# Sixteen of the adaLN dot products moved from the projections to the output projection and the down product

## The chip, the cores and the metric

The kernel runs on one core of one Trainium2 chip. The metric is device time in microseconds (us) of one launch. Of TensorE (PE), VectorE (DVE), ScalarE (ACT), GpSimd (POOL) and the queue that SyncE (SP) issues transfers on, each works through its own instruction list in order; a later instruction of a list never passes an earlier one that waits.

## The reference, cut to what matters

The program is one layer: an adaLN-modulated bidirectional mLSTM mixer, then an adaLN-modulated ConvFFN, over 1024 latent tokens of width 1024 with a prefix of 256 context tokens.

```
cx = silu(c)                                     # one row of 1024
sh1, sc1, g1, sh2, sc2, g2 = split(cx @ ada_w + ada_b, 6)     # 6 x 1024 values
hx = rmsnorm(x) * (1 + sc1) + sh1                # needed first of all
yx = mlstm_mixer(hx, hc) @ w_out                 # projections, scan, output projection
x  = x + g1 * rmsnorm(yx)                        # g1 is needed at the end of the output projection
hx = rmsnorm(x) * (1 + sc2) + sh2                # sh2, sc2: before the up product
yx = conv_ffn(hx)                                # up product, gate with convolution, down product
x  = x + g2 * rmsnorm(yx)                        # g2: only at the end of the down product
```

The change concerns the matrix-vector product cx @ ada_w. Its 6144 outputs are computed on DVE as 48 dot products: the weights of 128 outputs lie as a tile of 128 partitions by 1024 (512 KB), and one DVE instruction multiplies it with the row silu(c), which is held in every partition, and sums each partition into one column of a table (accs). The kernel numbers them so that 0 to 15 give sh1 and sc1, 16 to 23 sh2, 24 to 31 sc2, 32 to 39 g1 and 40 to 47 g2.

## The kernel before, in words

All large products are fp32 done as three fp32r matmuls (mm3, lines 172 to 174 and 179 to 181: high by high, high by low, low by high). An operand is split into its high half on ACT (whi, L167) and its low half on DVE (wlo, L168), so the third matmul of a weight block waits for DVE. Most products are cut into 2 by 2 blocks with Strassen-like sums; the sums of weight blocks are made on POOL (L359 for query/key/output-gate weights, L335 for value weights).

The program's stages, with the times of the profiled execution: startup and first quadrant of the projections (to about 85 us), the rest of the projections (to 330), the scan (to about 452), the output projection (452 to 540, two calls of out_gemm, L1478, each a sequence of units of 24 matmuls or so, with a plan of callbacks that run behind each unit), the up product with the gate (to 983), and the down product (983 to the end, 39 units with a plan of the same kind).

In the second half of the projections the tiles come in an order that is written out: A2_ORDER = [4, 5, ("v", 0), 6, ("v", 1), 7, 0, 1, 2, 3]. A number is a pair of query/key/output-gate column blocks (tile_pair), which multiplies the weights w3, w6, w7, w5, w4 in turn and adds the partial products on DVE (L1010, L1014, L1022). ("v", 0) and ("v", 1) are the two value pairs (v_pair), with sums of partial products at L937 and L966, a bias row vd = vd - vb on DVE (L960; both rows are loaded by L926 and L927) and an addition of that row on POOL (L961). During pair 7 the input gates are prepared (u_t, L868 to L873).

32 dots (16 to 47) are spread over these tiles: ADA says how many stand in which tile, and ada_rest (L814) issues at each of a few points a load on SP's queue (L822) and the dot on DVE (L441). The load goes into a free piece of the buffers V or QK, and the slot is written again by a later load. The last of them also makes the six modulation tables (A2, B2, G12).

```
ADA = {4: 4, 5: 4, ("v", 0): 8, 6: 3, ("v", 1): 6, 7: 7}
nc.sync.dma_start(raw, ada[u])                       # L822, SP's queue
ada_dot(raw, 0, accs[:, 4 + i:5 + i], raw)           # L441, DVE, 128x1024
```

Instructions come out in an order that a scheduler chooses from the written one (tc.high_priority moves the sums ahead), so a change of the written order can reorder instructions that it does not touch.

g_row (L1460 to L1466) spreads a gate of G12 into a row for the post-norm; for the mixer it runs ahead of the output projection, for the FFN behind unit 1 of the down product. In the output projection, turn and make_first prepare the first operand of the up product (xa0 and xa1, tiles A11 and A12) from the mixer's normalised result; AR is a 13312-wide scratch tile whose pieces serve the stages from there on.

## Time and profile before

| | |
|---|---|
| three runs, median (lowest, highest) | 1210.31 us (1207.49, 1213.03) |
| the profiled execution's own time | 1207.42 us |
| its span, first to last instruction | 1205.3 us |
| mean granted TensorE clock | 0.990 |
| PE busy, share of the span | 1159.3 us, 96% |
| DVE busy | 894.9 us, 74% |
| ACT busy | 555.4 us, 46% |
| POOL busy | 340.8 us, 28% |

The profile shows one execution. Busy shares are means over all stages; an engine that is busy three quarters of the whole can be the one that everything waits for in a stretch of it. The granted clock is the share of full speed that TensorE was given; 1.00 is 2.4 GHz, and its lower level is half of that, 1.2 GHz.

### The profile page before, as it was taken

To read this page: it belongs to the slowest core of one execution; us is meant where nothing else is said; L and a number is where in the kernel's file an instruction comes from. 1 tells how busy PE (TensorE), PEld (TensorE's weight loads), DVE (VectorE), ACT (ScalarE), POOL (GpSimd) and SP (SyncE) were. 2 spreads that over 40 slices of the span, in tenths; PEclk is the share of its full clock that TensorE was granted. 3 is DMA by queue.
4 is the path that set the end of the run, shared out by engine and by line. 5 is a ranking of instruction groups with operands and counts; after the bars stand their busy time and mean duration, and the time that the engine had idled before them with its cause. 6 is when DMAs were issued, how large, how long until landed. Compare 5 with 4: busy or idle time off the path is not lost.

```text
span 1205.3 us, 15889 instructions
## 1 busy us (share of the span) xinstructions
PE 1159.3 (96%) x5348; PEld 942.8 (78%) x5348; DVE 894.9 (74%) x1554; ACT 555.4 (46%) x1108; POOL 340.8 (28%) x286
## 2 busy tenths in 40 slices
PE   9999997897999989999989999999999999999997
PEld 6469887796878878887868888787788888888885
DVE  6987689989658787656976666888887887555664
ACT  3354332233257775668743443334334366444431
POOL 1045353524445442312233342233332400000000
PEclk8999999998999999999999999999999999999999
DMA  8977678766332469544475544665566589765461
GB/s 300 329 260 231 182 233 299 230 224 205 116 139 97 132 187 308 199 157 162 168 225 179 198 157 140 210 223 178 210 216 212 188 269 330 230 222 190 170 199 70
DMA packets 117042, 246.30 MB, mean 204 GB/s; under 512 B 11841, under 2 KB 28353, under 8 KB 116962
## 3 DMA queue, kind: packets, MB, share of 16 engines
q1 hardware_dynamic: 115762, 240.98, 59.6%
q0 software_dynamic: 1200, 4.33, 1.0%
q8 instruction: 42, 0.69, 0.2%
q14 instruction: 38, 0.31, 0.1%
HBM read 184.54 MB, written 60.72 MB: 203 GB/s over the span
## 4 chain that ended last, share of the span: by engine, by line
PE 40%; DVE 7%; ACT 4%; issue 3%; POOL 1%; DMA 0%; DVEq 0%; POOLq 0%; ACTq 0%
PE PS L172 14%; PE PS L174 13%; PE PS L173 13%; DVE wlo L168 2%; ACT whi L167 1%; DVE AR L1625 1%; DVE AR L1878 1%; DVE AR L1624 1%; ACT AR L1626 1%; ACT AR L1621 1%; POOL AR L1696 0%; DVE AR L2078 0%; DMA raw<-in_w_dram 0%; DVE PS L1864 0%; ACT xa L167 0%
## 5 line engine op out<-in xcount | busy, mean ns | idle before, releaser
L168 DVE TENSOR_TENSOR wlo<-raw,whi 128x512 fp32r<-128x512 f32 (+2 forms) x191 | 163.1, 875 | 121.9 <-ACT whi L167 121.6
L172 PE MATMUL PS<-xa,whi 128*128 128x512 f32 x616 | 244.3, 397 | 6.7 <-ACT AR L1852 5.2
L174 PE MATMUL PS<-xa,wlo 128*128 128x512 f32 x616 | 241.4, 392 | 1.1 <-DVE wlo L168 1.1
L173 PE MATMUL PS<-xa,whi 128*128 128x512 f32 x616 | 240.8, 391 | 0.0
L167 ACT CAST whi<-raw 128x512 fp32r<-128x512 f32 (+2 forms) x191 | 120.5, 656 | 152.3 <-PE PS L174 108.3
L172 PEld LDWEIGHTS PS<-xa,whi 128*128 128x128 f32 x616 | 115.9, 188 | 38.7 <-ACT AR L1852 8.0
L1696 POOL TENSOR_TENSOR AR<-raw 128x512 f32<-128x512 f32 x44 | 65.0, 1479 | 276.4 <-DMA raw<-in_w_dram 148.7
L174 PEld LDWEIGHTS PS<-xa,wlo 128*128 128x128 f32 x616 | 116.0, 188 | 27.5 <-DVE wlo L168 1.6
L173 PEld LDWEIGHTS PS<-xa,whi 128*128 128x128 f32 x616 | 116.1, 188 | 24.2
L172 PE MATMUL PS<-whi,xa 128*128 128x512 f32 x308 | 120.7, 392 | 0.0
L174 PE MATMUL PS<-whi,xa 128*128 128x512 f32 x308 | 120.6, 392 | 0.0
L173 PE MATMUL PS<-wlo,xa 128*128 128x512 f32 x308 | 120.6, 392 | 0.0
L168 DVE TENSOR_TENSOR wlo<-AR,whi 128x512 fp32r<-128x512 f32 x88 | 66.1, 757 | 59.4 <-ACT whi L167 59.4
L1626 ACT ACTIVATE AR<-AR 128x512 f32<-128x512 f32 x44 | 27.9, 635 | 132.7 <-DVE AR L1625 132.7
L2074 POOL TENSOR_TENSOR ss_m<-ss_m,mhalf 128x1 f32<-128x1 f32 x8 | 5.2, 651 | 231.1 <-DVE ss_m L2073 231.1
L172 PEld LDWEIGHTS PS<-whi,xa 128*128 128x128 f32 x308 | 57.9, 188 | 12.8
L174 PEld LDWEIGHTS PS<-whi,xa 128*128 128x128 f32 x308 | 57.8, 188 | 12.8
L173 PEld LDWEIGHTS PS<-wlo,xa 128*128 128x128 f32 x308 | 57.8, 188 | 12.8
L1696 POOL TENSOR_TENSOR AR<-raw,AR 128x512 f32<-128x512 f32 x44 | 66.5, 1510 | 1.7
L1621 ACT ACTIVATE AR<-PS,cols 128x512 f32<-128x512 f32 x44 | 34.2, 778 | 61.6 <-PE PS L174 42.4
L168 DVE TENSOR_TENSOR xa<-AR,xa 128x512 fp32r<-128x512 f32 x89 | 56.6, 685 | 7.5 <-ACT xa L167 7.4
L592 PE MATMUL PS<-XS,raw 128*128 128x512 f32 x128 | 55.2, 593 | 0.2 <-DVE XS L541 0.2
(424 smaller groups left out, 2542.4 us busy)
## 6 DMA issues: line engine op xcount, KB each, us to landing
raw<-in_w_dram SPq DMA_DIRECT2D x88, 512.0 KB, 4.0
asp<-AR SPq DMA_DIRECT2D x77, 256.0 KB, 3.9
AR<-asp SPq DMA_DIRECT2D x38, 512.0 KB, 5.0
AR<-in_w_dram SPq DMA_DIRECT2D x44, 256.0 KB, 4.1
bsp<-AR SPq DMA_DIRECT2D x44, 256.0 KB, 2.5
raw<-bsp SPq DMA_DIRECT2D x44, 256.0 KB, 3.3
V<-in_ada_dram SPq DMA_DIRECT2D x19, 512.0 KB, 5.6
raw<-in_w_dram SPq DMA_DIRECT2D x33, 256.0 KB, 3.4
```

The source lines that it names most:

```text
L167: act.copy(dst_hi, src)
L168: eng.tensor_tensor(dst_lo, src, dst_hi.bitcast(F32), op=ALU.subtract)
L172: pe.matmul(o, lh, rh, start=first, stop=False, skip_group_check=skip)
L173: pe.matmul(o, lh, rl, start=False, stop=False, skip_group_check=skip)
L174: pe.matmul(o, ll, rh, start=False, stop=last, skip_group_check=skip)
L592: pe.matmul(PS[:, m], wt[:, m * P:(m + 1) * P], xo, start=kt == 0, stop=kt % 4 == 3, skip_group_check=kt > 3)
L1621: act.activation(dst, src, AF.Identity, scale=cw[1], bias=cols[:, C_CB + f:C_CB + f + 1])
L1624: dve.scalar_tensor_tensor(c3[:, :, 1:], g3[:, :, :GW - 1], cw[0], c3[:, :, 1:], op0=ALU.mult, op1=ALU.add)
L1625: dve.scalar_tensor_tensor(c3[:, :, :GW - 1], g3[:, :, 1:], cw[2], c3[:, :, :GW - 1], op0=ALU.mult, op1=ALU.add)
L1626: act.activation(dst, dst, AF.Silu)
L1696: pool.tensor_tensor(d, x0, x1, op=ALU.subtract)
L1878: dve.tensor_tensor(d, x0, x1, op=ALU.subtract)
```

## The change

- `rest` keeps sixteen dots in the projections (16 to 19, 24 to 27, 32 to 39), and ADA places 2, 2, 4, 2, 3 and 3 of them where 4, 4, 8, 3, 6 and 7 stood.
- The row silu(c) is written to DRAM once (silsp, in the startup, SP's queue), since its tile is gone later on; SIL, a piece of AR, is filled from it in both later places by a load that spreads it over the partitions.
- Eight dots (20 to 23, 28 to 31) go to the output projection: the row and eight loads of 512 KB behind units 1 to 5 of the first call, into two tiles AX that take the buffers of A11 and A12; the dots behind units 6 to 9 of the first and 0 to 3 of the second call; then ada_first_rows(4, 8) makes the second half of A2 and B2. A11 and A12 are allocated after the dots that read their buffers.
- Eight dots (40 to 47, the FFN's gate) go to the down product: row and first loads behind units 1 to 5, the dots behind units 4 to 11, in four slots of AR. ada_gain(1) and g_row(1, 0) move from behind unit 1 to behind unit 13.

```
+    silsp = dram.tile([1, D], F32, name="silsp")
...
+            nc.sync.dma_start(silsp, sil[0][0:1])
...
-    rest = list(range(16, 48))
+    rest = list(range(16, 20)) + list(range(24, 28)) + list(range(32, 40))
...
-    ADA = {4: 4, 5: 4, ("v", 0): 8, 6: 3, ("v", 1): 6, 7: 7}
+    ADA = {4: 2, 5: 2, ("v", 0): 4, 6: 2, ("v", 1): 3, 7: 3}
...
+    def ada_further(units, slots):
+        def load(n):
+            if n < len(units):
+                nc.sync.dma_start(slots[n % len(slots)], ada[units[n]])
+
+        def row():
+            nc.sync.dma_start(SIL, silsp.broadcast_to([P, D]))
+
+        def dot(n):
+            raw, i = slots[n % len(slots)], units[n] - 16
+            dve.scalar_tensor_tensor(raw, raw, 1.0, SIL, op0=ALU.mult, op1=ALU.mult, accum_out=accs[:, 4 + i:5 + i])
+            load(n + len(slots))
+
+        return [row] + [lambda n=n: load(n) for n in range(len(slots))], [lambda n=n: dot(n) for n in range(len(units))]
+
+    begin, dots = ada_further([20, 28, 21, 29, 22, 30, 23, 31],
+                       [t[:, k] for t in AX for k in range(4)])
...
+    for n in range(9):
+        plan[1 + n // 2].append(begin[n])
+    for n in range(4):
+        plan[6 + n].append(dots[n])
     out_gemm(KT, lambda k, lo: yT(0, k, lo), plan, tail=2)
+    OPX = [operand(fpool, 0)]
...
+    for n in range(4):
+        plan[n].append(dots[4 + n])
+    plan[4] += [lambda: ada_first_rows(4, KT), lambda: OPX.append(operand(fpool, 1))]
...
-    plan[1].append(lambda: g_row(1, 0))
+    begin, dots = ada_further(list(range(40, 48)), [AR[:, q * 1024:(q + 1) * 1024] for q in range(4)])
+    for n, g in enumerate(begin):
+        plan[1 + n].append(g)
+    for n, g in enumerate(dots):
+        plan[4 + n].append(g)
+    plan[13] += [lambda: ada_gain(1), lambda: g_row(1, 0)]
```

Line numbers of the changed kernel are higher by 1 from line 157, by 2 from about 564 and by 13 from about 835, so L168 is L169 there, L960 L973, L961 L974, L966 L979, L1010 L1023 and L822 L841.

The first place is DVE's list from the third matmul's weights of pair 6 (wlo<-V is the low half of w6) to the sum L1010 behind them; QK is the buffer that holds the value pairs' sums, SPARE behind wlo is the weight block that follows. Before:

```order
L168 TENSOR_TENSOR wlo<-V_1044,whi 128x512
L168 TENSOR_TENSOR wlo<-raw,whi 128x512
L441 SCALAR_TENSOR_TENSOR V_1044,accs<-V_1044,SPARE 128x1024
L168 TENSOR_TENSOR wlo<-raw,whi 128x512 x2
L441 SCALAR_TENSOR_TENSOR V_1044,accs<-V_1044,SPARE 128x1024
...
L168 TENSOR_TENSOR wlo<-SPARE,whi 128x512
L960 TENSOR_TENSOR QK_1041<-QK_1041 128x256
L1010 TENSOR_TENSOR V_1044<-PS,V_1044 128x512
```

And in the changed kernel:

```order
L442 SCALAR_TENSOR_TENSOR V_1046,accs<-V_1046,SPARE 128x1024
L973 TENSOR_TENSOR QK_1043<-QK_1043 128x256
L169 TENSOR_TENSOR wlo<-V_1046,whi 128x512
L169 TENSOR_TENSOR wlo<-raw,whi 128x512
...
L169 TENSOR_TENSOR wlo<-raw,whi 128x512 x2
L981 TENSOR_TENSOR GT<-PS,QK_1043 128x16
L169 TENSOR_TENSOR wlo<-SPARE,whi 128x512
L1023 TENSOR_TENSOR V_1046<-PS,V_1046 128x512
```

No dot is left between the low half of w6 and the sum, and the subtraction of the second value pair's bias rows (L960, now L973) has moved from the end of this stretch to its head, ahead of the low half of w6.

The second place is POOL's list at the end of the first value pair; L961 is the bias addition of that pair, L359 are the weight sums of pair 6, L335 those of the second value pair. Before:

```order
L335 TENSOR_TENSOR QK_1042<-QK_1042,SPARE 128x544
L961 TENSOR_TENSOR QK_1041<-QK_1041 128x1088
L359 TENSOR_TENSOR raw<-raw 128x512 x2
L359 TENSOR_TENSOR V_1044<-raw 128x512
L359 TENSOR_TENSOR raw<-raw,V_1044 128x512
L335 TENSOR_TENSOR QK_1042<-QK_1042 128x512
```

And in the changed kernel:

```order
L336 TENSOR_TENSOR QK_1044<-QK_1044,SPARE 128x544
L360 TENSOR_TENSOR raw<-raw 128x512 x2
L360 TENSOR_TENSOR V_1046<-raw 128x512
L360 TENSOR_TENSOR raw<-raw,V_1046 128x512
L336 TENSOR_TENSOR QK_1044<-QK_1044 128x512
L336 TENSOR_TENSOR SPARE<-QK_1044 128x512
L336 TENSOR_TENSOR QK_1044<-QK_1044 128x512 x2
L974 TENSOR_TENSOR QK_1043<-QK_1043 128x1088
```

The bias addition has fallen behind eight weight sums. The load of the second value pair's bias row (L926, now L939), on which L973 waits, overwrites what L961 (now L974) reads, and waits for it.

The third place is SP's queue at the start of the down product; raw<-in_w_dram and raw<-bsp are weight blocks of the down units, AR<-asp is the left operand, which a later step splits. Before:

```order
L1800 DMA AR<-asp 128x2x512
L1451 DMA raw<-in_w_dram 128x512 x4
L1800 DMA AR<-asp 128x2x512
L1451 DMA raw<-in_w_dram 128x512
L1451 DMA raw<-bsp 128x512
```

And in the changed kernel:

```order
L1842 DMA AR<-asp 128x2x512
L1596 DMA AR<-silsp 128x1024
L1466 DMA raw<-in_w_dram 128x512 x2
L1593 DMA AR<-in_ada_dram 128x1024
L1466 DMA raw<-in_w_dram 128x512 x2
L1842 DMA AR<-asp 128x2x512
L1466 DMA raw<-in_w_dram 128x512
L1466 DMA raw<-bsp 128x512
L1593 DMA AR<-in_ada_dram 128x1024
```

The row and two loads of ada weights stand among the loads of the down weights; their slots are pieces of AR that the gate's last sums on DVE still use.

## Rows read from the trace of the kernel before

**Rows 1.** The page's first part: busy time of each engine, share, instructions.

```profile
PE 1159.3 (96%) x5348; PEld 942.8 (78%) x5348; DVE 894.9 (74%) x1554; ACT 555.4 (46%) x1108; POOL 340.8 (28%) x286
```

**Rows 2.** Waits of PE, 150 to 300 us: in total, times, longest.

```profile
PE PS L181 <- DVE wlo L168: 6.3, 4, 2.0
PE PS L172 <- DVE V L1010: 4.2, 2, 3.5
PE PS L873 <- DVE u_t L870: 4.1, 1, 4.1
```

**Rows 3.** Windows: length, PE, PEld, DVE, ACT, POOL busy (instructions), PEclk, DMA share, GB/s.

```profile
150.00:300.00 150.00, 131.75 (x776) 115.75 (x775) 138.10 (x241) 43.22 (x73) 63.03 (x37) 0.97 0.70 239
200.00:230.00 30.00, 21.17 (x118) 17.71 (x118) 30.00 (x35) 4.24 (x8) 24.04 (x13) 0.99 0.63 207
229.00:234.00 5.00, 4.62 (x14) 3.70 (x15) 5.00 (x10) 0.05 (x1) 0.00 (x0) 0.66 0.49 134
279.00:285.00 6.00, 6.00 (x17) 4.78 (x18) 6.00 (x12) 0.80 (x2) 0.00 (x0) 0.58 0.75 258
```

**Rows 4.** Timeline of PE: start, length, what, and the idle time before it.

```profile
217.62 0.50 PE L174 MATMUL PS<-XB,wlo 128*128 128x512 f32 x1 [1.58 <-DVE wlo L168]
...
229.38 0.69 PE L172 MATMUL PS<-XD,whi 128*128 128x512 f32 x1 [3.52 <-DVE V L1010]
...
278.93 0.47 PE L873 MATMUL PS<-ident,u_t 128*128 128x128 f32 x1 [4.10 <-DVE u_t L870]
```

**Rows 5.** Timeline of DVE, 219 to 229 us.

```profile
219.19 2.32 DVE L441 SCALAR_TENSOR_TENSOR V<-V,SPARE 128x1024 f32<-128x1024 f32 x1
...
221.44 3.46 DVE L168 TENSOR_TENSOR wlo<-raw,whi 128x512 fp32r<-128x512 f32 x2
224.82 1.21 DVE L441 SCALAR_TENSOR_TENSOR V<-V,SPARE 128x1024 f32<-128x1024 f32 x1
...
228.22 0.42 DVE L960 TENSOR_TENSOR QK<-QK 128x256 f32<-128x256 f32 x1
```

**Rows 6.** Timeline of DVE, 270 to 279 us.

```profile
270.25 1.22 DVE L441 SCALAR_TENSOR_TENSOR QK<-QK,SPARE 128x1024 f32<-128x1024 f32 x1
...
273.09 2.31 DVE L441 SCALAR_TENSOR_TENSOR QK<-QK,SPARE 128x1024 f32<-128x1024 f32 x1
...
275.93 1.67 DVE L441 SCALAR_TENSOR_TENSOR QK<-QK,SPARE 128x1024 f32<-128x1024 f32 x1
```

**Rows 7.** Groups by line on DVE, 199 to 224 us: busy, mean ns of one.

```profile
L441 DVE SCALAR_TENSOR_TENSOR V<-V,SPARE 128x1024 f32<-128x1024 f32 x5 | 12.3, 2468 | 0.0
L168 DVE TENSOR_TENSOR wlo<-raw,whi 128x512 fp32r<-128x512 f32 x4 | 7.0, 1770 | 0.0
```

**Rows 8.** The same groups, 183 to 199 us.

```profile
L441 DVE SCALAR_TENSOR_TENSOR V<-V,SPARE 128x1024 f32<-128x1024 f32 x6 | 7.3, 1221 | 0.8 <-DMA V<-in_ada_dram 0.8
L168 DVE TENSOR_TENSOR wlo<-QK,whi 128x544 fp32r<-128x544 f32 x5 | 3.6, 717 | 0.0
```

**Rows 9.** Timeline of POOL, 199 to 225 us, its first and last instruction.

```profile
199.09 2.53 POOL L961 TENSOR_TENSOR QK<-QK 128x1088 f32<-128x1088 f32 x1 [28.74 <-DVE V L937]
...
222.62 1.74 POOL L335 TENSOR_TENSOR QK<-QK,SPARE 128x512 f32<-128x512 f32 x1
```

**Rows 10.** Timeline of SP's queue, 187 to 195 us: the ada loads ahead of raw.

```profile
187.11 7.70 SPq L822 DMA_DIRECT2D V<-in_ada_dram  x4
194.90 0.38 SPq L353 DMA_DIRECT2D raw<-in_w_dram  x1
```

**Rows 11.** Line L926, the two loads of the bias row: issue to landing.

```profile
DMA to landing us min/median/max: 6.4/7.0/7.6
```

**Rows 12.** Windows of the output projection and of the first part of the down product.

```profile
460.00:480.00 20.00, 20.00 (x89) 16.54 (x89) 14.46 (x24) 10.36 (x20) 5.04 (x7) 1.00 0.97 348
480.00:520.00 40.00, 40.00 (x186) 33.36 (x185) 26.08 (x42) 27.43 (x46) 11.69 (x12) 1.00 0.66 240
960.00:1020.00 60.00, 60.00 (x271) 49.20 (x270) 49.58 (x77) 37.73 (x70) 4.34 (x3) 1.00 0.88 302
```

29 lines of the change are left out of this document (19 added, 10 removed).

## The prediction

> **What bounds the kernel now.** I began with the page's busy shares: PE works 1159.3 us of a span of 1205.3 [rows 1], so all that a rearrangement can win is some 46 us of idle PE, plus what a lowered clock costs. The next question is whether any of it lies where the sixteen dots come from. PE's waits between 150 and 300 us answer it: 6.3 us on the low halves of value weights (wlo, L181), 4.2 on the sum L1010 and 4.1 on u_t [rows 2], and 1.58 on the low half of w6 [rows 4], all released by DVE, 16.2 us together. The windows show the same from the other side: PE works 131.75 of these 150 us, and from 200 to 230 DVE is busy in all 30 us of 30 [rows 3]. DVE's 74% of the whole is here 100%, and DVE is what PE waits for.
>
> What DVE does ahead of each wait is read from its timeline. Ahead of the sum that releases PE at 229.38 after 3.52 idle [rows 4] stand dots of 2.32 and 1.21 us, two low halves in 3.46 us, and the bias subtraction L960 of 0.42 [rows 5]. Ahead of u_t, which releases PE at 278.93 after 4.10 [rows 4], stand dots of 1.22, 2.31 and 1.67 [rows 6]. The two waits have a second price. Behind each, TensorE is granted its lower level for a while: the mean clock is 0.66 from 229 to 234 and 0.58 from 279 to 285 [rows 3], while PE idle of 1.58 ahead of 217.62 [rows 4] leaves the clock of 200 to 230 at 0.99 [rows 3]. At half speed work takes twice as long, so 5 x 0.34 = 1.7 us and 6 x 0.42 = 2.5 us are lost there. So the two waits cost 3.5 + 1.7 and 4.1 + 2.5, together 11.8 us.
>
> **What is removed.** From the projections sixteen dots go. One costs 1.22 us of DVE where POOL is idle and 2.47 where it works [rows 8, 7], so 20 to 40 us of DVE, but only what ends on PE counts. I take the stretches in turn.
>
> *First value pair to w6* (before 217.62). In this stretch PE waits 6.3 us [rows 2] and 1.6 [rows 4], and about half of its dots leave, which alone would give up to 7.9. Against it stand the two reorderings that the second and the first place above show. POOL's weight sums for pair 6 now run before L961 instead of after it, so the contention that lifts a low half from 0.72 to 1.77 us [rows 8, 7] begins earlier, while its total stays. And DVE now has L960 ahead of the low half of w6. L960 waits for the bias row, the bias load waits for L961, and L961 comes after eight weight sums. L961 ran from 199.09 to 201.6, and twelve sums behind it until 224.4 [rows 9], 1.9 us each; eight of them are 15.2 us. They start when pair 6's raw weights are there, and those were issued at 194.90, behind ada loads that held SP's queue for 7.70 us waiting for slots [rows 10]. Half of these loads are gone, so I let the sums start 5 to 7 us ahead of L961's old start, at 192 to 194; eight sums and 2.53 for L961 then end at 210 to 212 if each keeps its 1.9 us, and some 3 us sooner, at 207, where DVE's shorter list meets fewer of them. The row lands 6.4 to 7.6 us behind its issue [rows 11], so at 214 to 219; with 0.42 for L960 and 1.77 for the low half, w6's third matmul comes between 216 and 221, where it came at 217.62. I take the earlier part of that, about 217.6, and so no change here: the gain of the value pair is absorbed by this wait. Bounds: 7.9 us gained if the wait is not last, 3.5 lost at its late end; more in the rivals.
>
> *w6 to w4.* From 219.19 to 228.55 the list held two dots and L960, 2.32 + 1.21 + 0.42 = 3.95 us [rows 5], and none of the three stands there now. The wait was 3.52, so it ends: gain 3.5 (bound below 2.5, if the two low halves of 3.46 lie later in POOL's contention), and with the idle time the drop of the clock, 1.7.
>
> *u_t in pair 7.* Of the dots ahead of u_t three go, 1.22 + 2.31 + 1.67 = 5.2 us [rows 6], against a wait of 4.10: gain 4.1 (bound below 2.3, if the dot that stays meets POOL), and 2.5 of clock. If 1 us or so of idle stays, the clock holds, as it does over the 1.58 above.
>
> **What is added.** *Startup*: one store of 4 KB on SP, a few tenths of a us on a queue that no PE wait there hangs on; 0. *Small DVE work*: six modulation instructions more, on rows of 4 to 8 columns; under 1 us, in stretches where DVE has room; 0 (bound 1).
>
> *Output projection.* Eight dots at 1.22 (POOL works only 11.69 of the 40 us from 480 to 520 [rows 12]) are 9.8 us of DVE, in a stretch where it is busy 26.08 of 40 and so has 13.9 free [rows 12]. PE never waits there (20.00 and 40.00 busy), so the weights are split ahead of it. The loads are 8 x 0.524 + 0.524 = 4.7 MB. From 460 to 480 the DMA engines are 0.97 busy at 348 GB/s, so they add about 4.7 MB / 348 GB/s = 13.5 us of transfer, which spreads over what comes next: 0.34 x 40 = 13.6 us are free from 480 to 520 [rows 12]. They fit, with nothing to spare. I take a loss of 0.5 us, bounds 0 and 6.
>
> *Down product.* PE is busy 60.00 of 60 from 960 to 1020, DVE 49.58, DMA 0.88 [rows 12]. Eight dots need 9.8 of the 10.4 us that DVE has free in the first 60, and some fall later. On SP two ada loads wait for DVE's last gate sums with weight loads of the down units behind them (third place). These loads run several units of some 5.5 us ahead of their use, so a delay of 4 or 5 us does not reach PE; 0, bounds 0 and 3. g_row moves from one unit to another and waits for dots that are long done; 0.
>
> **The sum.** 3.5 + 1.7 + 4.1 + 2.5 - 0.5 = 11.3 us. The profiled execution took 1207.42, so 1196.1; the median of the three runs is 1210.31, 2.9 above it, so 1199.0 against that median. I forecast 1199 us. Its own range is 1192 (the value pair's waits gone too) to 1204 (both lower bounds, and 2 us more in the output projection).
>
> **The rivals.** 0.5%, 6 us, is about what a measurement of this kernel can tell from no change: below 1204.3 is faster, above 1216.4 slower.
>
> *A: the wait on the bias row takes the place of the dots.* If L961 ends at 212 to 213, w6 comes about 4 us late, PE idles over 5 us in one piece, and the clock falls as after the 3.5 us at 229: 11.3 - 4 - 1.7 = 5.6 gained, 1204.7. For it: the new order itself, a first-in first-out list of eight sums and a load behind them. Against it: the value pair has room in DVE's shorter list. Chance 0.17.
>
> *B: the loads collide in the output projection.* With DMA at 0.97 and no slack, the operands of the second token half, which come over other queues at the same time, land late by about half of the 13.5 us, and PE waits some 6: 1205. Against it: PE idles nowhere from 460 to 520 now. Chance 0.13. The Trainium skill bears on this (DMA: Bandwidth & Descriptors, Issuing engines are not separate DMA queues): transfers that different engines issue run on the same 16 DMA engines and interleave, so the loads on SP's queue do delay those that POOL issues. The trace agrees so far as 0.97 busy is reached while both issue [rows 12].
>
> *C: the dots are not what makes DVE late.* Where POOL works (24.04 of the 30 us from 200 to 230 [rows 3]), every DVE instruction on two buffers takes 1.05 to 1.25 us longer [rows 7, 8]. If POOL's instructions pace DVE's, a removed dot only lets the next low half collide sooner, and the waits of low halves and sums stay; only the 1.67 + 1.22 of u_t's uncontended dots count: about 3, so 1207. Against it: a dot itself is one of the things that POOL slows, and three of them leave. Chance 0.12. The rule behind it is in the Trainium skill (SBUF — State Buffer, Who interferes with whom): a DVE instruction with two SBUF inputs contends with a GpSimd instruction that reads SBUF. By that rule the moved dots are also cheaper where they go, POOL being idle in most of both stages; the rows agree, 2468 against 1221 ns a dot [rows 7, 8].
>
> *D: slower.* The same wait as in A, but with L961 at the end of POOL's list, 222.62 + 1.74 = 224.4 [rows 9]. The row lands at 232, w6's third matmul comes at about 233.7, 16.1 later than now. The wait at w4 goes (3.5), the clock falls over a longer stretch (as much again as at 279, 2.5, against the 1.7 saved), u_t still gives 6.6: 16.1 - 3.5 + 0.8 - 6.6 = 6.8 lost, 1217. No gain is left from an end of L961 at about 217 on. For it: POOL's sums now wait for weights whose slots DVE frees. Against: eight sums at 1.9 us don't last from 194 to 222. Chance 0.08.
>
> **Chances.** The forecast 0.50, A 0.17, B 0.13, C 0.12, D 0.08. Nearly all of the forecast, under half of A and B and a little of C lie below 1204.3: faster 0.62; same 0.28; slower 0.10, which takes in that two losses meet. The range runs from 1191 to 1211: below, the value pair's 7.9 gained as well; above, all of C and what of A and B is worse than priced; D stays out.
>
> **What would show it.** Right: between w6 and w4 no PE wait, u_t's wait below 1 us, a granted clock of 1.00 over both stretches, dots of 1.2 us in the output projection and in the down product, PE busy throughout 460 to 520 and 985 to 1060. Wrong: a PE wait on the low half of w6 with DVE idle on the bias row (A, D); PE waits on the second token half's operands (B); low halves of 1.77 us and the old waits over the old 200 to 230 with fewer dots (C). The forecast also fails if a wait of over 3 us opens in a place where PE now has none, since that brings the clock down as well.

## The result and the profile after

The changed kernel takes 1192.15 us (median of 4 runs, 1190.73 to 1193.58), the kernel before beside it 1209.73 (4 runs, 1207.49 to 1213.03): a ratio of 0.9857, 95% interval 0.9838 to 0.9876. By the 0.5% that the prediction set as its bound, that is faster, as forecast, but the gain is 17.6 us against a forecast of 11.3, and the time lies just inside the lower end of the range.

The page's first part after, in the form of [rows 1]:

```profile
span 1191.8 us, 15884 instructions
...
PE 1155.9 (97%) x5348; PEld 941.3 (79%) x5348; DVE 898.7 (75%) x1561; ACT 556.2 (47%) x1108; POOL 343.8 (29%) x286
```

PE's busy time is 3.4 us less with the same 5348 matmuls, near the 4.2 us that the end of the two stretches at the lower clock should give (1.7 + 2.5). DVE works 3.8 us longer; its work was moved, not saved. The spans differ by 13.5 us. Most of the other 4 of the 17.6 comes from which execution was profiled: before, the profiled one (1207.42) was 2.3 below its median, and after, it (1193.58) was the slowest of four, 1.4 above.

To see where the 13.5 went I set the same matmul of both programs side by side and cut the span there. All marks are starts in PE's timeline, in us of the span. The one called an early matmul of the up product is its 13th, which waits for weights; it comes 3.3 us behind the very first (543.17 before, 529.53 after), so the differences are the same for either.

| mark | before | after | gained in the step |
|---|---|---|---|
| first sum of the second half of the projections (L1010 / L1023) | 158.78 | 159.32 | -0.5 |
| third matmul of w6 (L174 / L175) | 217.62 | 215.65 | 2.5 |
| first matmul of w4 (L172 / L173) | 229.38 | 223.49 | 3.9 |
| u_t (L873 / L886) | 278.93 | 266.63 | 6.4 |
| last transpose of pair 7 (L910 / L923) | 298.05 | 281.07 | 4.7 |
| g_row, end of the scan (L1465 / L1480) | 451.56 | 435.21 | -0.6 |
| an early matmul of the up product (L172 / L173) | 546.45 | 532.80 | -2.7 |
| end of the span | 1205.3 | 1191.8 | -0.2 |

So 16.9 us are gained between the first sum and the end of the scan (292.8 to 275.9), 2.7 are given back in the output projection (94.9 to 97.6), and behind it the two executions are alike (658.85 and 659.0): the eight dots in the down product cost nothing that shows here.

PE's waits from 140 to 290 us after, in the form of [rows 2] (total, times, longest):

```profile
PE PS L182 <- DVE wlo L169: 4.6, 4, 1.6
PE PS L173 <- DVE V L1023: 0.8, 1, 0.8
PE PS L175 <- DVE wlo L169: 0.5, 1, 0.5
```

The u_t wait of 4.1 is gone, and of the sums' waits only 0.8 is left, at the first mark of the table. Gone as well are two waits behind u_t, in the transposes at the end of pair 7, which [rows 2] leave out. PE's timeline before:

```profile
296.38 0.33 PE L909 MATMUL PS<-ident,QK 128*128 128x128 f32 x1 [0.71 <-DVE QK L899]
298.05 0.33 PE L910 MATMUL PS<-ident,QK 128*128 128x128 f32 x1 [1.34 <-ACT QK L905]
```

After, they start at 280.76 and 281.07 without a wait. The windows after, in the form of [rows 3] and [rows 12]:

```profile
215.00:230.00 15.00, 14.86 (x81) 12.62 (x80) 10.81 (x23) 4.67 (x8) 2.91 (x2) 1.00 0.60 204
260.00:285.00 25.00, 24.96 (x116) 20.40 (x115) 23.89 (x51) 11.41 (x20) 12.26 (x9) 1.00 0.53 158
...
460.00:500.00 40.00, 37.90 (x172) 30.87 (x172) 37.08 (x60) 23.58 (x39) 16.91 (x12) 1.00 0.79 297
968.00:1040.00 72.00, 72.00 (x315) 58.83 (x314) 60.12 (x100) 40.93 (x76) 0.00 (x0) 1.00 0.90 321
```

Around w4 and around u_t PE now works 14.86 of 15 and 24.96 of 25 us, at a granted clock of 1.00 where it had been 0.66 and 0.58. PE has no wait where it had two [rows 4], and its timeline shows two of the four smaller waits that are left in the value pair (the largest and the last):

```profile
200.00 0.39 PE L182 MATMUL PS<-wlo,XC 128*128 128x272 f32 x1 [1.63 <-DVE wlo L169]
...
208.54 0.39 PE L182 MATMUL PS<-wlo,XD 128*128 128x272 f32 x1 [0.98 <-DVE wlo L169]
...
215.65 0.50 PE L175 MATMUL PS<-XB,wlo 128*128 128x512 f32 x1
...
223.49 0.39 PE L173 MATMUL PS<-XD,whi 128*128 128x512 f32 x1
...
266.63 0.27 PE L886 MATMUL PS<-ident,u_t 128*128 128x128 f32 x1
```

DVE's timeline of the place that the forecast feared most, the bias subtraction L973 ahead of the low half of w6 (wlo<-V):

```profile
204.12 2.50 DVE L821 TENSOR_TENSOR accs<-accs,cols 128x4 f32<-128x4 f32 x1
206.65 1.20 DVE L823 SCALAR_TENSOR_TENSOR A<-accs,cols 128x4 f32<-128x4 f32 x1
207.77 0.71 DVE L169 TENSOR_TENSOR wlo<-QK,whi 128x544 fp32r<-128x544 f32 x1
...
212.34 2.31 DVE L442 SCALAR_TENSOR_TENSOR V<-V,SPARE 128x1024 f32<-128x1024 f32 x1
...
214.58 0.41 DVE L973 TENSOR_TENSOR QK<-QK 128x256 f32<-128x256 f32 x1
214.92 0.68 DVE L169 TENSOR_TENSOR wlo<-V,whi 128x512 fp32r<-128x512 f32 x1
...
219.58 0.68 DVE L1023 TENSOR_TENSOR V<-PS,V 128x512 f32<-128x512 f32 x1
```

L973 has no idle time ahead of it. The bias row was issued at 208.93 and there by 212.6; DVE, busy with L821 and two dots, came to L973 only at 214.58. POOL's timeline shows why the row is early enough:

```profile
203.56 3.02 POOL L974 TENSOR_TENSOR QK<-QK 128x1088 f32<-128x1088 f32 x1
...
209.60 3.97 POOL L336 TENSOR_TENSOR QK<-QK,SPARE 128x512 f32<-128x512 f32 x2
```

L974, which the bias load waits for, ends at 206.6, before the forecast's 210 to 212. The low half of w6 then ends at 215.60, 0.05 us before its matmul starts: DVE comes just in time. POOL's sums are over by 213.6, where they went on to 224.4 [rows 9], so low halves behind that take 0.68 us instead of 1.77 [rows 7].

In the output projection PE never waited before; now it does, twice (PE's timeline, 470 to 500 us):

```profile
486.88 0.50 PE L174 MATMUL PS<-wlo,YT 128*128 128x512 f32 x1 [1.28 <-DVE wlo L169]
...
493.43 0.50 PE L174 MATMUL PS<-wlo,YT 128*128 128x512 f32 x1 [0.82 <-DVE rs L416]
```

The issues of SP's queue there (434 to 494 us; count, KB each, median us from issue to landing) are the output weights (and eight new loads, with 10.6):

```profile
raw<-in_w_dram SPq DMA_DIRECT2D x8, 512.0 KB, 9.2
```

### The profile page after: what moved, and what is told of

The parts are those of the page before. It is cut to its first block, busy times and chain, and to the rows that moved or that the text cites. A ratio compares the mean times of both kernels' runs of the same rounds, so it can differ in the third digit from the quotient of the medians.

```text
span 1191.8 us, 15884 instructions
## 1 busy us (share of the span) xinstructions
PE 1155.9 (97%) x5348; PEld 941.3 (79%) x5348; DVE 898.7 (75%) x1561; ACT 556.2 (47%) x1108; POOL 343.8 (29%) x286
## 4 chain that ended last, share of the span: by engine, by line
PE 39%; DVE 8%; ACT 4%; issue 3%; DMA 1%; POOL 1%; DVEq 0%; POOLq 0%; ACTq 0%
PE PS L173 13%; PE PS L175 13%; PE PS L174 13%; DVE wlo L169 2%; ACT whi L168 1%; DVE AR L1667 1%; DVE AR L1920 1%; DVE AR L1666 1%; ACT AR L1668 1%; ACT AR L1663 1%; DVE PS L1906 0%; POOL AR L1738 0%; DVE AR L2120 0%; DMA raw<-in_w_dram 0%; DVE AR L1933 0%
## 5 line engine op out<-in xcount | busy, mean ns | idle before, releaser
L173 PE MATMUL PS<-xa,whi 128*128 128x512 f32 x616 | 244.3, 397 | 7.1 <-ACT AR L1894 5.4
L169 DVE TENSOR_TENSOR wlo<-raw,whi 128x512 fp32r<-128x512 f32 (+2 forms) x191 | 160.7, 861 | 109.1 <-ACT whi L168 106.7
L175 PE MATMUL PS<-xa,wlo 128*128 128x512 f32 x616 | 241.5, 392 | 1.1 <-DVE wlo L169 1.1
L174 PE MATMUL PS<-xa,whi 128*128 128x512 f32 x616 | 240.7, 391 | 0.0
L168 ACT CAST whi<-raw 128x512 fp32r<-128x512 f32 (+2 forms) x191 | 121.3, 656 | 145.4 <-PE PS L175 96.4
L173 PEld LDWEIGHTS PS<-xa,whi 128*128 128x128 f32 x616 | 116.0, 188 | 39.1 <-ACT AR L1894 8.1
L175 PEld LDWEIGHTS PS<-xa,wlo 128*128 128x128 f32 x616 | 116.0, 188 | 27.5 <-DVE wlo L169 1.6
L174 PEld LDWEIGHTS PS<-xa,whi 128*128 128x128 f32 x616 | 116.0, 188 | 24.2
L173 PE MATMUL PS<-whi,xa 128*128 128x512 f32 x308 | 120.7, 392 | 0.0
L175 PE MATMUL PS<-whi,xa 128*128 128x512 f32 x308 | 120.6, 392 | 0.0
L174 PE MATMUL PS<-wlo,xa 128*128 128x512 f32 x308 | 120.6, 392 | 0.0
L169 DVE TENSOR_TENSOR wlo<-AR,whi 128x512 fp32r<-128x512 f32 x88 | 67.7, 775 | 58.5 <-ACT whi L168 58.5
L174 PEld LDWEIGHTS PS<-wlo,xa 128*128 128x128 f32 x308 | 57.9, 188 | 12.8
L175 PEld LDWEIGHTS PS<-whi,xa 128*128 128x128 f32 x308 | 57.8, 188 | 12.8
L173 PEld LDWEIGHTS PS<-whi,xa 128*128 128x128 f32 x308 | 57.9, 188 | 12.7
L169 DVE TENSOR_TENSOR xa<-AR,xa 128x512 fp32r<-128x512 f32 x89 | 56.6, 683 | 4.9 <-ACT xa L168 4.9
```

The source lines that it names most:

```text
L168: act.copy(dst_hi, src)
L169: eng.tensor_tensor(dst_lo, src, dst_hi.bitcast(F32), op=ALU.subtract)
L173: pe.matmul(o, lh, rh, start=first, stop=False, skip_group_check=skip)
L174: pe.matmul(o, lh, rl, start=False, stop=False, skip_group_check=skip)
L175: pe.matmul(o, ll, rh, start=False, stop=last, skip_group_check=skip)
```

## The experiments

Every experiment was timed beside the kernel before on the same chip, so the ratios compare; medians of different chips do so less. Beside the ratio I read three stretches of each profiled execution, between the marks of the table above. The startup ahead of the first mark, which hardly differs between the kernels (a store of 4 KB, in e1 and e2 a memset), varies from 156.8 to 162.6 us between executions, so stretches are compared and not spans. Each stretch of the table is one execution. How far one can be trusted shows where kernels agree in it: e1, e2, e3, e5, e6 and e9 have the change's own projections, and the first stretch takes 273.8 to 275.9 us; e4, e7, e8 and e10 have its output projection, with 97.6 to 98.0; the last stretch varies by some 2 us either way without an edit in it.

| kernel | median us | ratio (95%) | first sum to g_row | g_row to up | rest |
|---|---|---|---|---|---|
| before | | | 292.8 | 94.9 | 658.9 |
| the change | 1192.15 | 0.9857 (0.9838 to 0.9876) | 275.9 | 97.6 | 659.0 |
| e1_left_out | 1188.43 | 0.9825 (0.9800 to 0.9849) | 274.7 | 94.9 | 659.9 |
| e2_out_loads | 1192.19 | 0.9857 (0.9833 to 0.9881) | 273.8 | 97.7 | 658.0 |
| e3_first8 | 1195.40 | 0.9885 (0.9858 to 0.9911) | 275.2 | 99.5 | 661.0 |
| e4_v0_none | 1197.20 | 0.9908 (0.9879 to 0.9936) | 278.9 | 97.6 | 657.7 |
| e5_dots_only | 1190.73 | 0.9854 (0.9830 to 0.9878) | 274.9 | 95.9 | 657.1 |
| e6_act_queue | 1204.57 | 0.9971 (0.9949 to 0.9993) | 274.2 | 110.6 | 659.1 |
| e7_v0_room | 1198.95 | 0.9915 (0.9895 to 0.9936) | 280.8 | 98.0 | 659.5 |
| e8_late_ada | 1197.97 | 0.9913 (0.9883 to 0.9944) | 281.0 | 97.7 | 657.8 |
| e9_late_loads | 1191.44 | 0.9848 (0.9823 to 0.9872) | 275.1 | 96.0 | 658.3 |
| e10_v0_sub | 1194.08 | 0.9871 (0.9847 to 0.9895) | 274.2 | 97.6 | 658.5 |
| e11_down_half | 1199.84 | 0.9920 (0.9893 to 0.9946) | 292.6 | 94.9 | 659.3 |
| e12_combined | 1188.14 | 0.9830 (0.9814 to 0.9846) | 274.6 | 95.9 | 661.3 |

### What do the additions cost, and where? (e1, e2, e5, e9)

**e1_left_out**: the moved dots, their loads and the row are gone from all places.

```diff
+    dve.memset(accs[:, 4:36], 0.0)
...
-    for n in range(9):
-        plan[1 + n // 2].append(begin[n])
-    for n in range(4):
-        plan[6 + n].append(dots[n])
...
-        plan[n].append(dots[4 + n])
...
-    for n, g in enumerate(dots):
-        plan[4 + n].append(g)
```

> The sixteen moved dots, their loads and the stored row are left out altogether (their columns of the table are zero, so shift, scale and the FFN's gate are incomplete); the sixteen that stay are where the change has them. Theory (the gain is made in the projections and about 2.7 us of it are given back in the output projection, none in the down product): 1189 to 1190, that is 2 to 3 us below the change's 1192.15, with no PE wait on low halves from 460 to 520. Rival (what is added costs nothing, the 2.7 us come from elsewhere): 1192, within 0.5. Rival (the down product also pays): under 1188.

Measured: the output projection is back at 94.9 us, the rest is not shorter (659.9), and the time is 1188.43. In that stretch the weights' loads take half as long to land as in the change:

```profile
raw<-in_w_dram SPq DMA_DIRECT2D x9, 512.0 KB, 4.6
```

What follows: what the additions cost is 2.7 us, in the output projection (3.7 by the medians, which are of different chips). The down product carries its eight dots and eight loads for nothing that shows within the 2 us. The removal alone gives the gain of the projections.

**e2_out_loads**: the eight dots of the output projection are left out, row and loads stay.

```diff
-    for n in range(4):
-        plan[6 + n].append(dots[n])
...
-    for n in range(4):
-        plan[n].append(dots[4 + n])
```

> The eight dots of the output projection are left out, their nine loads stay (half of the up product's shift and scale is incomplete); everything else as in the change. Theory (the two PE waits of 1.28 and 0.82 us on low halves come from dots in DVE's list ahead of them): both go, 1189 to 1190. Rival (the loads on busy DMA engines make the weights late): the waits stay, 1192.

Measured: 97.7, as in the change, with the same two waits (PE's timeline):

```profile
487.92 0.50 PE L175 MATMUL PS<-wlo,YT 128*128 128x512 f32 x1 [1.20 <-DVE wlo L170]
...
494.65 0.50 PE L175 MATMUL PS<-wlo,YT 128*128 128x512 f32 x1 [0.76 <-DVE wlo L170]
```

My theory, that the dots in DVE's list delay the low halves, falls: the loads make these waits without any dot. A part of the way is seen on SP's queue. In the change the low half that frees the next weight buffer ends at 461.38, but the load into it goes out only at 467.87, behind two ada loads at which SP stands, waiting for earlier transfers to land:

```profile
460.15 1.23 DVE L169 TENSOR_TENSOR wlo<-raw,whi 128x1024 fp32r<-128x1024 f32 x1
...
462.00 0.33 SPq L1593 DMA_DIRECT2D ax<-in_ada_dram  x1
465.68 0.33 SPq L1593 DMA_DIRECT2D ax<-in_ada_dram  x1
467.87 0.33 SPq L164 DMA_DIRECT2D raw<-in_w_dram  x1
```

So the weights are issued late and then take twice as long to land. The last step, from there to the two waits, is argued and not isolated: the low half that ends the wait at 487.92 runs from 485.55, stands behind steps of the post-norm in DVE's list, and takes 2.31 us beside POOL.

**e5_dots_only**: the other half. The dots stay and read the row itself in place of ada weights; the eight loads are left out.

```diff
-    def ada_further(units, slots):
+    def ada_further(units, slots, loads=True):
...
-            if n < len(units):
+            if loads and n < len(units):
...
-            dve.scalar_tensor_tensor(raw, raw, 1.0, SIL, op0=ALU.mult, op1=ALU.mult, accum_out=accs[:, 4 + i:5 + i])
+            dve.scalar_tensor_tensor(raw, raw if loads else SIL, 1.0, SIL, op0=ALU.mult, op1=ALU.mult, accum_out=accs[:, 4 + i:5 + i])
```

> The output projection's eight dots stay, but multiply the stored row with itself, and their eight loads of 512 KB are left out; the row's own load stays. The run before this one, loads without dots, kept the waits and the 97.7 us of the output projection (from the first g_row to the up product's first matmul; 94.9 without either). Theory (the loads cost, the dots are free): 94.9 to 95.4 us for this stretch, no PE wait over 0.3 between the two marks, 1189 to 1190 in all. Rival (either of the two is enough to make the low halves late): 97 us or more, 1192.

Measured: 95.9 us, one wait of 0.74 left. The theory that the dots are free was a little too good: dots and row cost 1.0, row and loads alone 2.8, all together 2.7. They overlap, and beside the loads the dots cost nothing more.

**e9_late_loads**: the loads go one behind each unit, where pairs went behind units 1 to 5.

```diff
-        plan[1 + n // 2].append(begin[n])
+        plan[1 + n].append(begin[n])
```

> As the change, but the nine loads of the output projection go out one behind each of units 1 to 9 instead of two, so that fewer weights stand behind them on SP's queue and DVE's list has the low halves of units 8 and 9 earlier. Theory (the loads ahead of the weights on one queue make the low halves late, and the list's order carries it on): the stretch from g_row to the up product falls from 97.6 us to 95 to 96, 1190 to 1191. Rival (the bytes themselves cost, wherever they stand): 97 us or more, 1192; or the last dots now wait for their loads and hold up the turn to the up product, 98 us or more.

Measured: 96.0 us and one wait of 0.73, as without the eight loads (e5). The weights' issues (434 to 494 us), and on SP's queue the load of e2's reading, which now goes out 0.02 us behind the low half that frees its buffer (it ends at 462.79):

```profile
raw<-in_w_dram SPq DMA_DIRECT2D x8, 512.0 KB, 7.6
```

```profile
462.81 0.33 SPq L164 DMA_DIRECT2D raw<-in_w_dram  x1
```

The same bytes cost 1.6 us less in the stretch when fewer of them stand ahead of a weight load. In the whole time the difference to the change (0.9848 against 0.9857) is too small for these runs to tell.

### Can the dots or the loads stand better? (e3, e6)

**e3_first8**: all eight dots behind units 6 to 9 of the first call.

```diff
-        plan[6 + n].append(dots[n])
+        plan[6 + n] += dots[2 * n:2 * n + 2]
...
-    for n in range(4):
-        plan[n].append(dots[4 + n])
```

> All eight dots of the output projection behind units 6 to 9 of its first call, two each, and none in the second call; nothing left out. Theory (a dot hurts where the low half behind it has little slack, in the first units of the second token half): waits of PE there shrink to 1 us or less, 1190 to 1191. Rival (the dots then wait for their loads and block DVE's list): waits of 3 us or more, 1193 to 1196.

Measured: 99.5 us in the stretch, 1195.4 in all, the time that the rival gave. The two waits of the change are gone, as in the theory, but two new ones open where the first operand of the up product is turned (1.83 and 0.71 us, PE's waits), and the granted clock falls behind them (499 to 506 us):

```profile
PE PS L1554 <- ACT HS L1567: 2.5, 2, 1.8
```

```profile
499.00:506.00 7.00, 6.03 (x26) 5.16 (x27) 3.07 (x4) 7.00 (x12) 0.00 (x0) 0.76 0.93 344
```

The waits are hardly longer than the change's; what makes the stretch 1.9 us longer is mostly the clock, 7 x 0.24 = 1.7 us. What follows: the second half of the dots is better in the second call.

**e6_act_queue**: row and loads of the output projection on the queue that ACT issues on.

```diff
-                nc.sync.dma_start(slots[n % len(slots)], ada[units[n]])
+                queue.dma_start(slots[n % len(slots)], ada[units[n]])
...
-            nc.sync.dma_start(SIL, silsp.broadcast_to([P, D]))
+            queue.dma_start(SIL, silsp.broadcast_to([P, D]))
...
-                       [t[:, k] for t in AX for k in range(4)])
+                       [t[:, k] for t in AX for k in range(4)], nc.scalar)
```

> As the change, but the row and the eight loads of the output projection are issued on ACT's queue instead of the one that the weights use. Theory 1 (the weights are late because they stand behind these loads in SP's queue): the stretch falls to about 95 us, 1189 to 1190. Theory 2 (they are late because the DMA engines are full): the stretch stays at 97 us or more, 1192. Either way ACT pays some tenths of a us for each issue.

Measured: 1204.57, and 110.6 us in the stretch. Neither theory fits. The raw weights do land sooner (6.1 us against 9.2, though they are issued at other times), but with the loads on another queue the scheduler put the dots earlier, ahead of operands that PE waits for. DVE's timeline and then PE's:

```profile
468.10 1.23 DVE L1600 SCALAR_TENSOR_TENSOR ax<-ax,AR 128x1024 f32<-128x1024 f32 x1 [11.03 <-DMA AR<-in_x_perm_dram]
```

```profile
474.81 0.79 PE L174 MATMUL PS<-wlo,YT 128*128 128x512 f32 x1 [7.77 <-DVE wlo L169]
...
480.94 0.79 PE L174 MATMUL PS<-wlo,YT 128*128 128x512 f32 x1 [3.21 <-DVE wlo L169]
```

The first dot waits 11.03 us, and everything behind it in DVE's list waits with it. The name shown is that of another load; the dot itself needs the row, which was issued at 454.44 and there by 464.2, and its ada weights, issued at 454.91 and there by 467.9. Behind the two waits the granted clock is 0.50 from 474 to 486. What the other queue alone would do stays open, since the order changed too.

### What holds PE in the value pairs, and the bias row (e4, e7, e8, e10)

**e4_v0_none**: no dot in the first value pair; its four go to the other tiles.

```diff
-    ADA = {4: 2, 5: 2, ("v", 0): 4, 6: 2, ("v", 1): 3, 7: 3}
+    ADA = {4: 3, 5: 3, ("v", 0): 0, 6: 2, ("v", 1): 4, 7: 4}
```

> The sixteen dots of the projections are placed anew: none beside the first value pair, 3, 3, 2, 4 and 4 beside tiles 4, 5, 6, the second value pair and 7. Theory (dots, not POOL's contention, make the low halves of the first value pair late): the 4.6 us of PE waits there shrink to 1 or 2, 1188 to 1190. Rival (POOL's weight sums pace DVE): the waits stay at 4 us or more, 1192 or over. Third possibility: the dots added beside tiles 4 and 5 open new waits there, 1192 to 1195.

Measured: the value pair's waits on its low halves shrink to one of 0.54, but the stretch is 3.0 us longer than in the change. (PS<-XC is w3, the weight block ahead of w6.) PE's and DVE's timelines and a window behind the wait:

```profile
209.39 0.79 PE L175 MATMUL PS<-XC,wlo 128*128 128x512 f32 x1 [4.24 <-DVE wlo L169]
```

```profile
208.31 0.42 DVE L973 TENSOR_TENSOR QK<-QK 128x256 f32<-128x256 f32 x1 [6.06 <-DMA QK<-in_vbias_in_dram]
```

```profile
209.00:216.00 7.00, 6.61 (x23) 5.36 (x24) 5.49 (x16) 0.62 (x1) 2.58 (x2) 0.76 0.80 269
```

Two things follow. The waits in the value pair go with the dots while POOL's sums stay, so POOL alone doesn't make them. And rival A's wait is real: with the dots gone DVE comes to L973 before the row has landed, stands for 6.06 us with the low halves of w3 and w6 behind it, and PE idles 4.24 at w3's, after which the clock falls (0.76 over 7 us, 1.7 us lost).

**e7_v0_room**: e4, and the second value pair's bias row gets a place of its own, so that its load need not wait for L974.

```diff
-    return U, Z, QK[0][:, 2176:2176 + n], QK[0][:, 2448:2448 + n]
+    return U, Z, QK[0][:, (2176, 2720)[p_]:][:, :n], QK[0][:, 2448:2448 + n]
```

> The placement of the fourth run (no dots beside the first value pair), and the second value pair's bias row gets a place of its own, so that its load no longer waits for POOL's addition. Theory (in the fourth run DVE stood 6.06 us at the bias row's subtraction, and that made the wait of 4.24 us and the lower clock behind it): that wait goes, and the stretch from the first sum at about 158 us to the first g_row falls from the fourth run's 278.9 us by 4 to 6, to 273 to 275, below the change's 275.9; 1187 to 1189 in all. Rival (POOL's sums pace DVE, another wait of that size takes its place): 277 us or more.

Measured: no better (280.8, the rival's sign). DVE's timeline, then PE's:

```profile
193.50 0.67 DVE L973 TENSOR_TENSOR QK<-QK 128x256 f32<-128x256 f32 x1 [5.05 <-DMA QK<-in_vbias_in_dram]
```

```profile
207.59 0.60 PE L182 MATMUL PS<-wlo,XD 128*128 128x272 f32 x1 [4.08 <-DVE wlo L169]
```

With its load free to start earlier, the scheduler moves L973 forward too, 15 us, again to where the row has not landed. DVE is late from there on, and two dots of 2.31 and 3.52 us in POOL's contention follow ahead of the low half that PE waits for at 207.59; how much of that wait is the stop and how much POOL's contention was not separated. The theory that the shared place makes DVE's stop falls; what makes it is that an instruction nobody hurries for stands in DVE's in-order list and waits for a load.

**e8_late_ada**: dots moved late, seven in pair 7.

```diff
-    ADA = {4: 2, 5: 2, ("v", 0): 4, 6: 2, ("v", 1): 3, 7: 3}
+    ADA = {4: 1, 5: 1, ("v", 0): 2, 6: 1, ("v", 1): 4, 7: 7}
```

> The same sixteen dots stay in the projections, but 1, 1, 2, 1, 4 and 7 of them beside tiles 4, 5, the first value pair, 6, the second and 7, so that as many stand ahead of u_t as before the change. Theory (dots in DVE's list ahead of u_t make its wait, and the wait lowers the clock): a PE wait of 3 to 4 us at u_t, a mean clock of 0.6 to 0.7 in the 6 us behind it, 5 to 6 us in all against what the fewer dots of the first value pair give. Rival (u_t was late because the whole of DVE's list was, from the value pair on): no wait at u_t above 1 us.

Measured: 281.0. The bias row's wait is there again (L973 idle 5.56 us on DVE; PE 3.71 at 211.15). The theory's wait at u_t did not come (the rival's sign); the transposes behind it are late, and the clock from 275 to 285 falls to 0.66:

```profile
277.59 0.30 PE L896 MATMUL PS<-ident,QK 128*128 128x128 f32 x1 [1.67 <-DVE QK L889]
```

```profile
275.00:285.00 10.00, 7.42 (x22) 5.50 (x21) 9.77 (x21) 5.06 (x8) 4.90 (x4) 0.66 0.63 191
```

So seven dots in pair 7, four of them ahead of u_t, don't bring u_t's wait back; DVE is late one step behind it. PE itself was 3.71 us and some clock late by then, which gives DVE time, so this doesn't show which of the removed dots had made u_t's wait.

**e10_v0_sub**: e4, and the subtraction of the bias row on POOL.

```diff
-        dve.tensor_tensor(vd, vd, vb, op=ALU.subtract)
+        pool.tensor_tensor(vd, vd, vb, op=ALU.subtract)
```

> The placement of the fourth run, with the subtraction of the bias rows on POOL, ahead of POOL's addition, instead of on DVE. Theory (what stopped DVE in the fourth, seventh and eighth run, for 6.06, 5.05 and 5.56 us, is that this instruction stands in DVE's list where its row has not landed): DVE has no such stop, PE no wait over 2 us between the first value pair and pair 7, and the stretch from the first sum to g_row is 273 to 275 us (278.9 in the fourth run, 275.9 in the change). Rival (the value pair's low halves are late for another reason): a wait of 3 us or more stays, 277 us or over.

Measured: 274.2; e4's wait of 4.24 is gone. PE's waits from 150 to 290 us:

```profile
PE PS L922 <- DVE QK L912: 1.7, 1, 1.7
PE PS L923 <- ACT QK L918: 1.2, 1, 1.2
PE PS L173 <- DVE V L1023: 0.8, 1, 0.8
PE PS L182 <- DVE wlo L169: 0.3, 1, 0.3
```

Of four waits in the value pairs, 4.6 us together, 0.3 is left, and u_t comes 101.0 us behind the first sum where it took 107.3 in the change. Of these 6.3 us, 3.2 are given back by the end of pair 7 (L922, L923), where one dot more stands than in the change, and 1.4 by the end of the scan. The latter fits the clock, which falls behind these two waits (5 x 0.34 = 1.7 us; 275 to 280 us):

```profile
275.00:280.00 5.00, 4.57 (x14) 3.63 (x15) 3.46 (x8) 1.32 (x4) 0.73 (x1) 0.66 0.48 121
```

Against e4, which differs by this line alone, the stretch is 4.7 us shorter, of the 5.9 that the wait and the clock behind it had cost. Against the change, 274.2 is no gain that can be told: it lies within the 273.8 to 275.9 that the change's own projections take, the whole time is no better (0.9871 against 0.9857), and the profiled execution was its fastest.

### The halves together (e11, e12)

**e11_down_half**: only the FFN gate's dots leave the projections; 24 stay and the output projection is as before.

```diff
-    rest = list(range(16, 20)) + list(range(24, 28)) + list(range(32, 40))
+    rest = list(range(16, 40))
...
-    ADA = {4: 2, 5: 2, ("v", 0): 4, 6: 2, ("v", 1): 3, 7: 3}
+    ADA = {4: 3, 5: 3, ("v", 0): 6, 6: 2, ("v", 1): 5, 7: 5}
```

> Only the down product's half of the change: 24 dots stay in the projections (3, 3, 6, 2, 5 and 5 beside the tiles) and none goes to the output projection. Theory (waits that end on a dot shrink dot by dot, the two big ones and their clock go as soon as half of the moved dots have left): the stretch from the first sum to g_row is 278 to 284 us (292.8 before, 275.9 in the change), the output projection 94.9; 1194 to 1200 in all. Rival (all sixteen are needed before anything moves, since POOL's list or a load sets the pace): 288 us or more, 1205 or over. Rival (eight are enough): 277 or less, under 1193.

Measured: 1199.84 (nine runs, 1196.32 to 1208.12), some six tenths of the change's gain, as the theory had it (at its upper end). The output projection stands at 94.9. The stretch of the projections and the scan measured 292.6, outside the theory's 278 to 284, but the profiled execution was one of the two slowest (1206.73): an event in the scan that is told at the end holds PE for 6.33 us and the clock at 0.50 for 6 us behind it. Without these 9.3 us it would be about 283 (an estimate). u_t comes 109.1 us behind the first sum, where it took 120.2 before and 107.3 in the change.

**e12_combined**: the subtraction on POOL, the loads one per unit, and two dots in the first value pair.

```diff
-    ADA = {4: 2, 5: 2, ("v", 0): 4, 6: 2, ("v", 1): 3, 7: 3}
+    ADA = {4: 3, 5: 3, ("v", 0): 2, 6: 2, ("v", 1): 3, 7: 3}
...
-        dve.tensor_tensor(vd, vd, vb, op=ALU.subtract)
+        pool.tensor_tensor(vd, vd, vb, op=ALU.subtract)
...
-        plan[1 + n // 2].append(begin[n])
+        plan[1 + n].append(begin[n])
```

> The change with three edits: the subtraction of the bias rows on POOL, the output projection's loads one behind each unit (as in the ninth run), and the dots of the projections 3, 3, 2, 2, 3 and 3 beside the tiles, so that the first value pair has two and pair 7 no more than in the change. Theory (each edit removes what its own run showed: the low halves of the value pair, DVE's stop at the bias row, the loads ahead of the weights; and dots behind u_t, which cost the tenth run 3 us between u_t and the scan, are not added): 271 to 274 us from the first sum to g_row (275.9 in the change, 274.2 in the tenth run), 96 to the up product (97.6), 1187 to 1189 in all. Rival (the gains ahead of u_t are given back behind it, whatever stands there): 275 or more, 1191 to 1192.

Measured: 1188.14 (6 runs, 1185.99 to 1194.54), 0.9830 of the kernel before. Its median lies 4 us below the change's, but the two were timed on different chips and their intervals (to 0.9846, from 0.9838) just overlap. The stretch from the first sum to g_row, 274.6, missed its 271 to 274 and is no shorter than the change's projections take elsewhere. PE no longer waits for the bias row (on POOL the second pair's subtraction starts at 215.99, without idle time), and of the two waits in the output projection one is left:

```profile
486.73 0.50 PE L174 MATMUL PS<-wlo,YT 128*128 128x512 f32 x1 [0.75 <-DVE wlo L169]
```

## Why the prediction was right, and where it was off

*Where the dots stood.* Right. DVE's list was what PE waited for, and with the dots gone (e1 shows that the removal alone does it) the two waits and their two stretches at the lower clock are gone. "w6 to w4" was priced at 3.5 and gave 3.9; the clock behind it (1.7) and u_t's wait (4.1) together 5.8 and gave 6.4; the clock behind u_t 2.5, which is in the 4.7 of the next step. These four terms, 11.8 us, came as worked out, the last by the granted clock (1.00 from 260 to 285), since the step holds other work too. Which dots had made u_t's wait is less sure than the prediction has it: it counted those just ahead of u_t, and e8, with four of seven dots of pair 7 there, has no such wait.

*"First value pair to w6": no change.* Off by 2.5 us, within its bounds. The wait on the bias row was taken to be last there. It was not, for two reasons that the rows after show: L974 ended at 206.6 rather than 210 to 212, since POOL's sums began at 190.2 rather than 192 to 194 and the eight took 13.4 us rather than 15.2, and the row took 3.7 us to land, not 6.4 to 7.6 [rows 11]. DVE's own list was still full until then: it reached the subtraction after the row. The low half behind it took 0.68 us, not the assumed 1.77, as POOL was done. So about 2.5 of the 7.9 us that the pair had to give were gained. Rival A did not decide here, but e4, e7 and e8 show that it was close: in each of them DVE reached L973 5 to 6 us before its row, and PE had a wait of 3.7 to 4.2 us behind that and lost some clock.

*A term that was missing.* The rest of the step behind u_t, 4.7 - 2.5, is the transposes of pair 7: they had waited 0.71 and 1.34 us for DVE and for ACT behind it, and now don't. The view that [rows 2] are cut from has both, 1.3 and 0.7 us, below the three groups shown; the prediction put them at nothing.

*"I take a loss of 0.5 us" in the output projection.* This is the term that was mis-sized: it measured 2.7, within its bounds of 0 to 6. Its working added up DVE's free time and the DMA engines' free time, and both sums were sound. What it left out is the order on SP's queue. Ada loads stand ahead of weight loads there; one weight load goes out 6.5 us behind the low half that frees its buffer, and the weights land 9.2 us behind their issue instead of 4.6 (e1). e2 shows that the loads make the waits without any dot, e5 that the dots and the row alone cost 1.0, e9 that with the same loads spread over more units the stretch costs no more than that. The step from late weights to the two late low halves is argued. Rival B, which had the second half's operands late by about 6 us, saw the right stretch, but neither the transfer nor the size.

The Trainium skill (DMA: Bandwidth & Descriptors, Issuing engines are not separate DMA queues) says that transfers run on the same 16 engines and interleave whoever issues them. The trace agrees as far as the ada loads slow the weight loads beside them (9.2 us to landing against 4.6). That the order on the queue has a part of its own shows in the late issue and in e9, not in e6, whose weights were issued at other times.

*Down product and startup.* Both 0, and both were: PE works 72.00 of 72 us from 968 to 1040, with the dots in it, and e1, without them, is no faster there. The startup moved by -0.5, less than it varies by itself.

*"Small DVE work": 0, bound 1.* Nearer its bound. DVE has seven instructions more, not six (1561 against 1554). L821 and L823, on four columns, took 2.50 and 1.20 us beside L974 on POOL, and stand directly ahead of the low half whose matmul waits 0.98 at 208.54. That they make this wait was not isolated.

*Rival C*, POOL as the pace-maker, is refuted: e4 and e10 leave POOL's sums as they are and take the dots out, and the value pair's waits go from 4.6 us to 0.5 and 0.3. The contention itself is real: beside POOL a dot took 2.31 us, and the four-column addition L821 2.50, where its shortest instance takes 0.15. So the rival's 1.05 to 1.25 us more for every instruction on two buffers is too narrow. The Trainium skill (SBUF — State Buffer, Who interferes with whom) states that a DVE instruction with two SBUF inputs contends with a GpSimd instruction that reads SBUF; the trace agrees. Contention lengthens what stands in the list; the list is what PE waits for. *D* did not come: POOL's list, not only L974, was done by 213.6.

*The signs.* Of what would show it right, no wait between w6 and w4, none at u_t, the clock of 1.00 and PE busy from 985 to 1060 (75.00 of 75 us) came. Two did not: PE works 57.90 of the 60 us from 460 to 520, and three of the eight dots there took 2.13 to 2.25 us, beside POOL, where 1.2 was assumed.

*The number.* The sum in spans was 11.3 and measured 13.5: +2.5 value pair, +2.2 transposes, about +1 on the priced waits, less 2.2 in the output projection, 0.6 in the scan, 0.5 in the startup and 0.2 behind it. Each of these is from one execution, and the first stretch alone differs by 2.1 us between executions of the same projections. Between the medians 3.7 us more lie in which execution each profile caught (2.3 and 1.4). That part no view of the one execution could give. So the time came inside the range partly by luck: terms that were off by 2.5, 2.2 and 1 one way and by 3.5 the other way cancel in part, and the low end of the range stood for something else, the value pair's whole 7.9 us (1199.0 - 7.9 is 1191.1, as in the range of the chances; the 1192 given beside the sum doesn't follow from it).

## What to carry to other kernels

Where an engine is busy all the time in one stage, take work off its list there and not from the mean; what counts there is what ends on PE, and the stretch at the lower clock that followed the waits here. When work is put elsewhere, its loads count as much as its instructions: ask what they stand ahead of on the in-order queue, and spread them. And look in each in-order list for a small instruction that waits for a load with urgent ones behind it: removing the work ahead of it uncovers that wait, so move it to an engine that isn't waited for (in e10 the wait went with that, though the kernel as a whole got no faster than the change).

## What the runs showed of the hardware

A DVE instruction was held for some twenty times its length. In the profiled execution of e11, in the scan, a low half of 128 x 256 elements, whose shortest instance is 0.38 us, took 7.50 us (DVE's timeline), and PE then waited 6.33 (PE's):

```profile
351.85 7.50 DVE L169 TENSOR_TENSOR wlo<-raw,whi 128x256 fp32r<-128x256 f32 x1 [0.25 <-ACT whi L168]
```

```profile
359.81 1.23 PE L1096 MATMUL PS<-V,SA 128*128 128x257 f32 x2 [6.33 <-DVE SA L1104]
```

POOL ran instructions of 0.73 us back to back from 342.65 to 359.08, and the DVE instruction ended some 0.3 us behind the last of them. That fits its being shut out for some ten POOL instructions in a row, not for one. Behind PE's wait the granted clock is at its lower level (359 to 365 us):

```profile
359.00:365.00 6.00, 5.19 (x14) 4.27 (x15) 3.95 (x12) 2.00 (x7) 0.08 (x1) 0.50 0.03 12
```

The execution shows it once; why this instance and no other, stays open.

The clock followed waits as in the trace before: after PE's wait of 4.24 us (e4) the granted clock was 0.76 from 209 to 216. But the length of one wait doesn't tell it. Behind two waits close together it fell where neither was long: 1.83 and 0.71 us in e3 (0.76 from 499 to 506), 1.74 and 1.25 in e10 (0.66 from 275 to 280). In e4 the same two, 1.75 and 1.25, left it at 1.00 (280 to 285), and so did single waits of up to 1.63 in the change. The prediction's sign, a wait of over 3 us, would have missed e3 and e10.

The startup, up to the first mark, took 156.8 to 162.6 us in the fourteen profiled executions, almost 6 us, though almost the same instructions run there (a store of 4 KB and, in e1 and e2, a memset apart).
